# Order of the seven weight sums, the place of three loads, and the engine of some adds, in a one-layer streaming encoder on one core

## The chip, the cores and the metric

The kernel runs on one NeuronCore of one Trainium2 chip. The metric is the device time of one execution in microseconds (us). A core has five engines that work side by side, each through its own queue in order: TensorE (PE; its weight loads are shown as PEld), VectorE (DVE), ScalarE (ACT), GpSimd (POOL) and SyncE (SP). Nearly all transfers between the chip's main memory and the on-chip memory are issued from SP's queue.

## What is computed

One layer over 1024 prompt tokens and 64 sample tokens, handled as one matrix of 1088 columns: a combined projection, retention with four heads, sliding-window attention, a gated merge, cross-attention over 256 memory tokens, and a SwiGLU with an inner width of 2816, each with an RMS norm before it. All in float32. Cut to what matters here:

```
def mixer_prompt(h, g_attn, w_in, w_ret_out, w_swa_out, w_mix_out, sinks, bias, log_gamma):
    rq, rk, rv, rg, sq, sk, sv, ga, gb = in_proj(h, g_attn, w_in)
    q, k, v = retention_qkv(rq, rk, rv, pos)
    ret_state, o = lax.scan(lambda st, xs: retention_block(st, xs[0], xs[1], xs[2], log_gamma),
                            s0, (blk(q), blk(k), blk(v)))
    swa_o = swa_attend(q_s, band_blocks(k_s), band_blocks(v_s), bias, sinks, valid)
    y = merge_branches(ret_o, rg, swa_o, ga, gb, w_ret_out, w_swa_out, w_mix_out)

def swiglu(x, g_ffn, w_gate, w_up, w_down):
    hn = rms_norm(x, g_ffn)
    return (jax.nn.silu(hn @ w_gate) * (hn @ w_up)) @ w_down

hp = hp + y
hp = hp + cross_attn(hp, mk, mv, g_cross, w_cq, w_co)
hp = hp + swiglu(hp, g_ffn, w_gate, w_up, w_down)
```

## The kernel before

**Precision.** Each float32 operand is split in two halves (`split`, L122 to L124): ACT casts the high half (L123), DVE subtracts it from the source for the low half (L124). A product is then three matmuls: high by high, high by low, low by high (L212, L213 and L215 in `multiply`).

**Seven products instead of eight.** The large projections multiply a weight block of 2 by 2 parts with an activation block of 2 by 2 parts through seven products (`strassen`, L254). TensorE makes them in the order P1, P2, P6, P5, P7, P3, P4. Their activation operands are B11, B21, T2, T1, T3, B22 and T4, in that order: the B are parts of the activation, the T sums of such parts. A product of the full size is 24 matmuls of 128x128 by 272 columns, one of the last row group 18. The results are combined on DVE (`add` inside `strassen`, L259), and `emit`, which each caller writes, takes them out. In the profile the weight operands are called `wq`, the activation operands B, b or T (the digits of a name are left out there), and the result in PSUM `pq`.

**The weight operands.** `weight_ops` (L173) receives two tiles `raw` (two buffers in all; one holds a11 and a12, the other a21 and a22). Four sums are made in place on POOL (L190, L191, L193, L196), and each of the seven operands is split by `put` into a tile `wq` from `new_op` (five buffers, and a sixth one in a pool of its own from a certain point on). The order written is P1, P2, P7, P6, P5, P3, P4. P7 is a11 - a21; P6 is a22 - P7 and overwrites it, so it waits until P7 has been split; P5 is a21 + a22; P3 is a12 - P6. The argument `ahead` of `new_op` tells only the bookkeeping of the sixth buffer that products are used in another order than that of the splits. This function runs for each of 59 weight sets. The first pass of the projection and the first passes of two row groups use `plain` instead: eight products of the unsummed parts, with weights from `plain_weights`, and no sums.

**Order.** The program is traced once; a scheduler then orders the instructions of each queue by a simulated timeline, starting from the order of the text. `with tc.issue_after(ins):` makes what the block issues on the queue of `ins` follow `ins` on that queue.

**The start.** `start_phase` loads x in 16 pieces (`xr`, four buffers), scales them by the gain on ACT into `xg`, and makes the B and T operands. The values of head 0 (`values(first, 0, self.plain)`, L658) are the first product round, a `plain` one; its four results are stored to `d_qkv` through tiles `early`. The next line, L659, loads the two tiles of w_k for head 0 and makes their weight operands.

**The down projection.** `down` (L1556) multiplies w_down with the hidden values, which were stored earlier as operands in `d_op`. It runs over three row groups of 8, 8 and 6 blocks (gi = 0, 1, 2) and in each over four column pairs (m = 0, 2, 4, 6). In a pass the two `raw` tiles of w_down are loaded (`load_half`, L1594 to L1596), then the products follow. For gi = 0 and 1 the pass with m = 0 is a `plain` one, and after it the operands T2, T1, T3 and T4 of the group are loaded (`load_operand`, through tiles `hl` by `fetch`, L1548) for the passes after it. In the last pass of a group `refill` loads the next group's operand into each slot that has become free. Each result is added to y in `add` (L1563): what comes from PSUM on DVE (L1566), what comes from an on-chip sum (u1, u3, u5) on POOL (L1568) in the first two groups and on DVE in the last one.

Of the kernel before, what the change touches and what calls it, by code (L numbers as in the profile page):

```python
# [2 lines left out]

# [1 line left out]

# [16 lines left out]
KT = D // P  # L22
# [20 lines left out]
OPS = ("B11", "T1", "T2", "B21", "T3", "B22", "T4", "B12")  # L43
# [66 lines left out]
class Kernel:  # L110
# [8 lines left out]
    def store(self, out, in_):  # L119
        self.nc.sync.dma_start(out, in_)  # L120
# [20 lines left out]
            parts += [(q[:, 0, i:i + width], q[:, 1, i:i + width]) for i in range(0, w, width)]  # L141
        return parts

    def new_op(self, ahead=0):

        self.turns += 1
        turn = self.turns + ahead
        if self.sixth is not None and self.last_held < min(self.held):
            self.last_held = turn
            return self.sixth.tile([P, 2, 512], F32R, tag="wq", bufs=1, name="wq")  # L150
        self.held = sorted(self.held)[-4:] + [turn]
        return self.wp.tile([P, 2, 512], F32R, tag="wq", bufs=5, name="wq")
# [20 lines left out]
    def weight_ops(self, raws, n=512, skip=()):  # L173

        nc = self.nc
        half = [[raws[i][:, j * n:(j + 1) * n] for j in range(2)] for i in range(2)]
        (a11, a12), (a21, a22) = half
        add, sub = ALU.add, ALU.subtract
        w = {}

        def put(name, src):
            if name in skip:
                return
            q = w[name] = self.new_op({"P7": 2, "P6": -1, "P5": -1}.get(name, 0))
            self.split(src, q[:, 0, :n], q[:, 1, :n])

        tt = nc.gpsimd.tensor_tensor
        put("P1", a11)
        put("P2", a12)
        tt(out=a11, in0=a11, in1=a21, op=sub)  # L190
        tt(out=a21, in0=a21, in1=a22, op=add)  # L191
        put("P7", a11)
        tt(out=a11, in0=a22, in1=a11, op=sub)  # L193
        put("P6", a11)
        put("P5", a21)
        tt(out=a12, in0=a12, in1=a11, op=sub)  # L196
        put("P3", a12)
        put("P4", a22)
        return w
# [372 lines left out]
    def project_phase(self):  # L572
        nc, tc, io = self.nc, self.tc, self.io
        with ExitStack() as ctx:
# [7 lines left out]
            first = self.start_phase(sctx)  # L582
# [3 lines left out]
            half = lambda t: slice(t * HALF, (t + 1) * HALF)  # L586
            flat = lambda o: o.rearrange("p b c -> p (b c)")

            def staged():
                count[0] += 1  # L590
                return stage[(count[0] - 1) % len(stage)]

            def taken(ps, sb):
                o = staged()
                if sb is None:
                    nc.scalar.copy(o, ps)
                else:
                    nc.vector.tensor_tensor(out=o, in0=ps, in1=sb, op=ALU.add)  # L598
                return flat(o)
# [39 lines left out]

            def values(w, h, by=self.strassen):  # L640
                def emit(i, t, ps, sb):
                    self.store(self.d_qkv[2, 2 * h + i, :, half(t)], taken(ps, sb))
                by(w, self.ops, emit)

            pair = lambda w, h: self.load_ops([io[w][2 * h + i] for i in range(2)])
            def queries(p):
# [8 lines left out]
                        self.store(d[:, 9:17, :], r(o[:, 32:]))  # L655
                return put

            values(first, 0, self.plain)  # L658
            first = pair("w_k", 0)  # L659
            sctx.close()  # L660
            stage, count = self.stage_tiles(), [0]
            with ExitStack() as rctx:
# [24 lines left out]
            for idx, w, act in ((1, "w_ga", AF.Sigmoid), (0, "w_rg", AF.Silu), (2, "w_gb", AF.Sigmoid)):  # L687
                for m in range(0, KT, 2):
                    if (idx, m) == (1, 6):
# [4 lines left out]
                        op = ctx.enter_context(tc.tile_pool(name="op", bufs=1, reuse_waits="tile"))  # L694
# [4 lines left out]
                    put = lambda i, t, o, idx=idx, m=m, store=store: store(self.d_gate[idx][m + i, :, half(t)], o)  # L699
# [848 lines left out]
    def fetch(self, name, group):  # L1548
        n0 = sum(GROUPS[:group]) // 2
        for k in range(GROUPS[group] // 2):  # L1550
            self.pools = self.pools[1:] + self.pools[:1]
            a = self.pools[0].tile([P, HALF], F32, tag="hl", name="hl")
            self.load(a, self.d_op[OPS.index(name), n0 + k])
            yield a

    def down(self, starts):  # L1556
        nc, io = self.nc, self.io
        self.rings[0].next = (self.rings[0].next - 2) % KT
        stage = self.ring_tiles(0, 2, "y", F32)
        y = [self.rstd_f] + [stage[i // 2][:, i % 2, :] for i in range(4)]  # L1560
        y += [self.yp.tile([P, T], F32, name=f"y{i}") for i in range(3)]
        half = lambda m, t: y[m][:, t * HALF:(t + 1) * HALF]
        def add(m, i, t, ps, sb, by=nc.gpsimd):  # L1563
            v = half(m + i, t).rearrange("p (b c) -> p b c", b=2)
            if ps is not None:
                nc.vector.tensor_tensor(out=v, in0=ps, in1=v, op=ALU.add)  # L1566
            if sb is not None:
                by.tensor_tensor(out=v, in0=sb, in1=v, op=ALU.add)  # L1568

        begun = set()  # L1570

        def complete(m, c0, n):
            acc, o = self.rstd[:, c0:c0 + n], y[m][:, c0:c0 + n]
            if c0 not in begun:
                begun.add(c0)
                nc.scalar.activation(acc, o, AF.Square)
            else:
                sq = self.hl.tile([P, HALF], F32, tag="hl", name="sq")[:, :n]
                nc.scalar.activation(sq, o, AF.Square)
                nc.vector.tensor_tensor(out=acc, in0=acc, in1=sq, op=ALU.add)  # L1580

        def load_half(tile, m, a, b):
            self.load(tile.rearrange("p (k m) -> p k m", m=P), io["w_down"][m, :, a:b, :])

        for gi, g in enumerate(GROUPS):
            last = gi == len(GROUPS) - 1
            f0, n = starts[gi], g * P // 2
            for m in range(0, KT, 2):
                def emit(i, t, ps, sb, m=m):
                    add(m, i, t, ps, sb, nc.vector if last else nc.gpsimd)  # L1590
                    if last and t == 1:
                        complete(m + i, HALF, HALF)

                raws = [self.wp.tile([P, 1024], F32, tag="raw", bufs=2, name="raw") for i in range(2)]  # L1594
                for i in range(2):
                    load_half(raws[i][:, :2 * n], m + i, f0, f0 + g)  # L1596
                if m == KT - 4 and not last:
                    for name in ("B11", "B21" if gi == 0 else "T2"):
                        self.ahead[name, gi + 1] = list(self.fetch(name, gi + 1))
                if gi == 0:  # L1600
                    for i in range(2):
                        self.load(y[m + i], self.d_h[1][m + i])
                if m == 0 and not last:
                    self.plain(self.plain_weights(raws, n), self.ops, emit)
                    for name in ("T2", "T1", "T3", "T4"):
                        self.load_operand(name, gi)
                else:
                    w = self.weight_ops(raws, n, ("P2", "P4") if last else ())
                    if m == KT - 2 and not last:
                        self.refill = lambda name, gi=gi: self.turn(name, 1) if gi == 0 else self.turn_last(name)  # L1610
                    self.strassen(w, self.ops, emit, last)
                    self.refill = None
                    if m == 0:
                        for name in ("B21", "T4"):
                            self.load_operand(name, gi)
                if last and m == KT - 4:
                    nc.scalar.activation(self.root[:, 0, :1], self.rstd[:, HALF:HALF + 1], AF.Sqrt)
        rest = []
        for m in range(0, KT, 2):
            raw = self.wp.tile([P, 1024], F32, tag="raw", bufs=2, name="raw")  # L1620
            for i in range(2):
                load_half(raw[:, i * n:(i + 1) * n], m + i, f0 + g // 2, f0 + g)
            ring, slots = self.slots["B11" if m < 4 else "T1"]
            q = self.rings[ring].tile("wb", slot=slots[m // 2 % 2])
            self.last_queued = self.split(raw[:, :2 * n], q[:, 0, :2 * n], q[:, 1, :2 * n])
            rest += [(m + i, q[:, :, i * n:(i + 1) * n], self.ops[("B21", "T4")[i]]) for i in range(2)]
        self.finish(y, rest)
# [205 lines left out]
```

## Time and profile before

| | us |
|---|---|
| median of 3 runs | 2198.7 |
| lowest and highest | 2195.81, 2199.74 |
| the profiled execution's own time | 2201.3 |
| its span, first to last instruction | 2198.7 |

The profile is of one execution. A row of the timeline gives the start, the duration, the engine (a small q after it marks the engine's queue, as for an issued transfer), the line, the operation, the tiles as out<-in, the shapes and xcount; brackets tell how long the engine stood idle before it, and what ended that. A row of busy times by stretch gives the stretch and its length, then for PE, PEld, DVE, ACT and POOL the busy time and the number of instructions, then the mean granted clock of TensorE, the busy share of the transfer engines and GB/s. A row of the waits gives who waited for whom, the total, the number of times and the longest. A row of the chain of waits gives start, duration and what it was. A row of the groups gives the mean duration in ns after the busy time; a row of one line's instructions gives the shortest, the median and the longest.

### The profile page before, as it was taken

How to read it: one execution, taken by the hardware profiler on the slowest of the kernel's cores; microseconds unless marked ns; L12 is line 12 of the kernel's file. 1: busy time of each engine (PE TensorE's matmuls, PEld its weight loads, DVE VectorE, ACT ScalarE, POOL GpSimd, SP SyncE). 2: the span in 40 equal slices, each digit the busy share in tenths (PEclk: the TensorE clock that was granted, in tenths of full speed). 3: DMA queues.
4: the chain of work that ended last, by engine and by line, in shares of the span. 5: the costliest groups of instructions: out<-in, count | busy, mean ns of one | idle time of the engine just before them, and what ended most of it. 6: DMA issues, size and time to landing. Idle time of an engine off the chain costs nothing.

```text
span 2198.7 us, 41701 instructions
## 1 busy us (share of the span) xinstructions
PE 2151.3 (98%) x16389; PEld 2096.3 (95%) x16389; DVE 1566.3 (71%) x2650; ACT 877.2 (40%) x1898; POOL 658.1 (30%) x506
## 2 busy tenths in 40 slices
PE   8999999999999999999999999999999999999997
PEld 8999999999999997889999999999999999999997
DVE  8996968776677658766454565768777777777588
ACT  7343424344344456653233343333222222334243
POOL 1222333342344113330000000015556556424441
PEclk9999999999999999999999999999999999999999
DMA  5534354435354467327443111422342332475333
GB/s 199 167 123 128 99 150 123 133 112 158 104 161 161 166 207 243 114 80 220 121 156 115 40 49 58 149 82 90 124 147 88 104 123 91 131 291 164 96 105 119
DMA packets 181444, 290.83 MB, mean 132 GB/s; under 512 B 40290, under 2 KB 109314, under 8 KB 181250
## 3 DMA queue, kind: packets, MB, share of 16 engines
q1 hardware_dynamic: 176130, 278.18, 40.1%
q10 hardware_dynamic: 4608, 8.36, 1.0%
q8 instruction: 129, 2.11, 0.4%
q0 software_dynamic: 512, 1.64, 0.2%
q14 instruction: 65, 0.53, 0.1%
HBM read 196.95 MB, written 91.16 MB: 131 GB/s over the span
## 4 chain that ended last, share of the span: by engine, by line
PE 77%; DVE 11%; DMA 5%; issue 3%; ACT 3%; POOL 1%; SPq 0%; POOLq 0%; DVEq 0%; ACTq 0%
PE pq L215 15%; PE pq L213 15%; PE pq L212 15%; PE pd L156 7%; PE pd L158 7%; PE pd L157 7%; DVE wq L124 2%; DMA hl<-d_op 1%; PE pout L1038 1%; DVE T L124 1%; DVE B L124 1%; PE pss L970 1%; DMA raw<-w_k 1%; PE pp L1014 1%; DMA qs<-d_qkv 1%
## 5 line engine op out<-in xcount | busy, mean ns | idle before, releaser
L123 ACT CAST wq<-raw 128x512 fp32r<-128x512 f32 (+1 forms) x499 | 303.8, 614 | 593.2 <-PE pq L215 243.2
L124 DVE TENSOR_TENSOR wq<-raw,wq 128x512 fp32r<-128x512 f32 (+1 forms) x499 | 440.8, 886 | 137.5 <-ACT wq L123 135.7
L212 PE MATMUL pq<-T,wq 128*128 128x272 f32 x1832 | 491.7, 288 | 4.5 <-ACT wq L123 3.1
L213 PE MATMUL pq<-T,wq 128*128 128x272 f32 x1832 | 492.5, 289 | 0.0
L213 PE MATMUL pq<-B,wq 128*128 128x272 f32 x1592 | 430.1, 290 | 8.0 <-DVE B L124 8.0
L212 PE MATMUL pq<-B,wq 128*128 128x272 f32 x1592 | 427.6, 289 | 2.3 <-DVE stage L598 2.0
L215 PE MATMUL pq<-T,wq 128*128 128x272 f32 x1832 | 382.9, 289 | 0.0
L190 POOL TENSOR_TENSOR raw<-raw 128x512 f32<-128x512 f32 (+1 forms) x59 | 79.0, 1339 | 968.7 <-DVE rs_r L301 482.9
L212 PEld LDWEIGHTS pq<-T,wq 128*128 128x128 f32 x1832 | 344.9, 188 | 6.5 <-ACT wq L123 2.9
L213 PEld LDWEIGHTS pq<-T,wq 128*128 128x128 f32 x1832 | 344.8, 188 | 0.8 <-issue 0.7
L215 PE MATMUL pq<-B,wq 128*128 128x272 f32 x1592 | 333.4, 290 | 0.0
L213 PEld LDWEIGHTS pq<-B,wq 128*128 128x128 f32 x1592 | 300.9, 189 | 10.6 <-DVE B L124 9.7
L212 PEld LDWEIGHTS pq<-B,wq 128*128 128x128 f32 x1592 | 300.4, 189 | 3.2 <-ACT wq L123 2.7
L215 PEld LDWEIGHTS pq<-T,wq 128*128 128x128 f32 x1832 | 290.5, 190 | 0.5 <-issue 0.3
L215 PEld LDWEIGHTS pq<-B,wq 128*128 128x128 f32 x1592 | 253.4, 190 | 0.8 <-issue 0.8
L259 DVE TENSOR_TENSOR u<-pq,u 128x544 f32<-128x544 f32 x177 | 127.2, 719 | 99.1 <-PE pq L215 98.9
L193 POOL TENSOR_TENSOR raw<-raw 128x512 f32<-128x512 f32 (+1 forms) x59 | 83.5, 1415 | 125.7 <-DVE wq L124 120.6
L598 DVE TENSOR_TENSOR stage<-pq,u 128x544 f32<-128x544 f32 x112 | 80.2, 716 | 34.7 <-PE pq L215 31.7
L191 POOL TENSOR_TENSOR raw<-raw 128x512 f32<-128x512 f32 (+1 forms) x59 | 90.8, 1539 | 3.5
L196 POOL TENSOR_TENSOR raw<-raw 128x512 f32<-128x512 f32 (+1 forms) x59 | 83.0, 1406 | 4.4
L1486 POOL TENSOR_TENSOR stage<-stage,rstd_f 128x544 f32<-128x544 f32 x40 | 63.9, 1607 | 39.1 <-ACT stage L1485 39.1
L156 PE MATMUL pd<-xc,wq 128*128 128x256 f32 (+1 forms) x256 | 74.5, 291 | 0.0
(385 smaller groups left out, 4575.9 us busy)
## 6 DMA issues: line engine op xcount, KB each, us to landing
hl<-d_op SPq DMA_DIRECT2D x85, 272.0 KB, 4.3
d_qkv<-stage SPq DMA_DIRECT2D x44, 272.0 KB, 2.6
d_op<-stage SPq DMA_DIRECT2D x44, 272.0 KB, 2.1
d_op<-ht SPq DMA_DIRECT2D x44, 272.0 KB, 3.3
raw<-w_gate SPq DMA_DIRECT2D x22, 512.0 KB, 3.6
raw<-w_up SPq DMA_DIRECT2D x22, 512.0 KB, 4.0
raw<-w_down SPq DMA_DIRECT2D x16, 512.0 KB, 4.5
d_gate<-stage ACTq DMA_DIRECT2D x28, 272.0 KB, 3.0
```

Source lines behind the costliest of these rows:

```text
L123: self.last_cast = self.nc.scalar.copy(hi, src).ins
L124: return self.nc.vector.tensor_tensor(out=lo, in0=src, in1=hi.bitcast(F32), op=ALU.subtract).ins
L156: mm(ps, wh, xh, start=start, stop=False)
L157: mm(ps, wh, xl, start=False, stop=False)
L158: self.last_mm = mm(ps, wl, xh, start=False, stop=stop).ins
L191: tt(out=a21, in0=a21, in1=a22, op=add)
L193: tt(out=a11, in0=a22, in1=a11, op=sub)
L196: tt(out=a12, in0=a12, in1=a11, op=sub)
L212: mm(ps[:, c, :HC], w[:, 0, ks], x[:, 0, cs], start=start, stop=False)
L213: mm(ps[:, c, :HC], w[:, 0, ks], x[:, 1, cs], start=False, stop=False)
L215: self.last_mm = mm(ps[:, c, :HC], w[:, 1, ks], x[:, 0, c * HC:(c + 1) * HC], start=False, stop=stop).ins
L259: add = lambda out, a, b: nc.vector.tensor_tensor(out=out, in0=a, in1=b, op=ALU.add)
```

## The change

- `weight_ops`: the sums and splits are rewritten. a21 + a22 comes first and needs nothing but the second `raw` tile. P6 is then (a21 + a22) - a11, once P1 has been split. P3's sum follows, and P7 comes last as a22 - P6, once P6 has been split and P3's sum is made. The splits stand in the order of the products. There are four sums on POOL and seven splits as before. `new_op` loses its argument.
- The w_k loads of head 0 follow the first store of the values on SP's queue. For that, `values` keeps its stores (through `load`, which issues the same transfer and returns it).
- In the down projection, for gi = 0 and 1, the w_down loads of m = 2 follow the last load of operand T1 on SP's queue. `fetch` keeps each load, and the loop remembers T1's.
- In the last pass (m = 6) of the first two groups the adds of on-chip sums to y go from POOL to DVE: four in each pass, eight in all.

```
-    def new_op(self, ahead=0):
+    def new_op(self):
 
         self.turns += 1
-        turn = self.turns + ahead
+        turn = self.turns
...
-            q = w[name] = self.new_op({"P7": 2, "P6": -1, "P5": -1}.get(name, 0))
+            q = w[name] = self.new_op()
             self.split(src, q[:, 0, :n], q[:, 1, :n])
 
         tt = nc.gpsimd.tensor_tensor
         put("P1", a11)
+        tt(out=a21, in0=a21, in1=a22, op=add)
         put("P2", a12)
-        tt(out=a11, in0=a11, in1=a21, op=sub)
-        tt(out=a21, in0=a21, in1=a22, op=add)
+        tt(out=a11, in0=a21, in1=a11, op=sub)
+        put("P6", a11)
+        tt(out=a12, in0=a12, in1=a11, op=sub)
+        put("P5", a21)
+        tt(out=a11, in0=a22, in1=a11, op=sub)
         put("P7", a11)
-        tt(out=a11, in0=a22, in1=a11, op=sub)
-        put("P6", a11)
-        put("P5", a21)
-        tt(out=a12, in0=a12, in1=a11, op=sub)
         put("P3", a12)
         put("P4", a22)
...
-                    self.store(self.d_qkv[2, 2 * h + i, :, half(t)], taken(ps, sb))
+                    self.stores.append(self.load(self.d_qkv[2, 2 * h + i, :, half(t)], taken(ps, sb)))
...
+            self.stores = []
             values(first, 0, self.plain)
-            first = pair("w_k", 0)
+            with tc.issue_after(self.stores[0]):
+                first = pair("w_k", 0)
...
-            self.load(a, self.d_op[OPS.index(name), n0 + k])
+            self.loaded = self.load(a, self.d_op[OPS.index(name), n0 + k])
...
-                    add(m, i, t, ps, sb, nc.vector if last else nc.gpsimd)
+                    add(m, i, t, ps, sb, nc.vector if last or m == KT - 2 else nc.gpsimd)
...
-                for i in range(2):
-                    load_half(raws[i][:, :2 * n], m + i, f0, f0 + g)
+                with self.tc.issue_after(self.loaded) if m == 2 and not last else nullcontext():
+                    for i in range(2):
+                        load_half(raws[i][:, :2 * n], m + i, f0, f0 + g)
...
                         self.load_operand(name, gi)
+                        if name == "T1":
+                            behind = self.loaded
+                    self.loaded = behind
```

More of the change, by code (lines that the diff above doesn't have):

```diff
@@ L1 @@
 import math
-from contextlib import ExitStack, contextmanager
+from contextlib import ExitStack, contextmanager, nullcontext
 import numpy as np
```

## The prediction

> **What bounds the kernel now.** I began with the page's head and its busy times, then asked who TensorE waited for, then took busy times by stretch, and last read the timeline of each queue where TensorE had stood still.
>
> ```profile
> span 2198.7 us, 41701 instructions
> PE 2151.3 (98%) x16389; PEld 2096.3 (95%) x16389; DVE 1566.3 (71%) x2650; ACT 877.2 (40%) x1898; POOL 658.1 (30%) x506
> ```
> ```profile
> PE pq L213 <- DVE B L124: 8.0, 6, 2.9
> PE pq L212 <- ACT wq L123: 3.1, 3, 1.3
> ```
> ```profile
> 9.00:41.00 32.00, 27.98 (x201) 26.57 (x200) 31.07 (x46) 26.47 (x46) 3.33 (x2) 0.95 0.48 162
> 47.00:120.00 73.00, 68.68 (x530) 67.47 (x531) 69.85 (x121) 30.84 (x53) 20.27 (x14) 0.98 0.51 164
> 1540.00:1595.00 55.00, 55.00 (x444) 55.00 (x443) 42.08 (x51) 16.39 (x28) 30.26 (x22) 1.00 0.37 124
> 2015.00:2040.00 25.00, 21.25 (x145) 20.49 (x144) 20.55 (x26) 11.82 (x21) 10.43 (x7) 0.86 0.80 255
> 2135.00:2150.00 15.00, 13.09 (x89) 12.57 (x88) 14.06 (x23) 4.66 (x9) 5.42 (x5) 0.89 0.19 53
> ```
>
> TensorE bounds it: 47.4 us of the span are left without a matmul, and no schedule can win more than that and the half-speed clock behind the holes. The stretch 1540 to 1595 gives the full rate: 444 matmuls in 55 us, 0.124 us each, so a product of 24 matmuls takes 2.97 us and one of 18 (the last group) 2.23 us. By that rate the other stretches show what three places lose: 201 matmuls are 24.9 us of 32, a loss of 7.1 us at the start; 145 are 18.0 us of 25, a loss of 7.0 us where the down projection passes from its first row group to its second; 89 are 11.0 us of 15, a loss of 4.0 us in the last group. The second loss is 3.75 us of idle time and, with a mean clock of 0.86, 3.5 us of slowness. The two wait rows name the causes: operand halves that VectorE (DVE) finishes late, and split weights.
>
> **The start (gate on the w_k loads).**
>
> ```profile
> 12.79 0.38 SPq L117 DMA_DIRECT2D raw<-w_k  x1
> 14.49 0.76 SPq L117 DMA_DIRECT2D raw<-w_k  x1
> ```
> ```profile
> 32.05 0.83 SPq L120 DMA_DIRECT2D d_qkv<-early  x2
> ```
> ```profile
> 19.75 0.69 DVE L124 TENSOR_TENSOR wq<-raw,wq 128x512 fp32r<-128x512 f32 x1
> 20.36 0.72 DVE L1393 TENSOR_TENSOR xg<-xg 128x544 f32<-128x544 f32 x1
> 20.99 1.81 DVE L124 TENSOR_TENSOR T<-xg,T 128x544 fp32r<-128x544 f32 x1
> 22.73 1.78 DVE L124 TENSOR_TENSOR B<-xg,B 128x544 fp32r<-128x544 f32 x1
> ```
> ```profile
> 20.52 1.70 POOL L190 TENSOR_TENSOR raw<-raw 128x512 f32<-128x512 f32 x1 [20.07 <-DVE wq L124]
> 22.30 1.63 POOL L191 TENSOR_TENSOR raw<-raw 128x512 f32<-128x512 f32 x1
> ```
> ```profile
> 24.57 0.60 PE L213 MATMUL pq<-B,wq 128*128 128x272 f32 x1 [2.86 <-DVE B L124]
> 47.89 0.39 PE L212 MATMUL pq<-T,wq 128*128 128x272 f32 x1 [1.20 <-ACT wq L123]
> ```
>
> Today 1 MB of w_k goes out at 12.79 and 14.49 us, among the last loads of x. Its first split and its first two sums then fall between 19.75 and 24 us, and DVE's operands beside the sums take 1.81 and 1.78 us where a free one takes 0.72: 2.15 us lost, and 0.69 for the split. The B half that frees TensorE ends at 24.51; without these 2.84 us it would end at 21.67, and the 2.86 us hole begins at 21.71. After the change both loads stand on SP behind the first store (32.05). The x loads behind them come earlier, and nothing of w_k is on DVE or POOL before the store. DVE then has x work of its own (31.07 of 32 us busy), so I expect a second hole to stay, and take half of the 7.1 us.
>
> What the delay puts at risk is w_k itself. P1 of the first product round starts two products and the hole before 47.89: 47.89 - 1.20 - 5.94 = 40.75 us. From the store at 32.05:
>
> ```profile
> 72.49 5.04 DMA raw<-w_k
> ```
> ```profile
> 311.50 11.98 DMA raw<-w_k
> ```
>
> A w_k transfer of 5.04 us ends at about 37.5, and the split (0.69, and a cast of about that length before it) leaves 1.9 us to spare; store and P1 move together when the holes go. At 11.98 us it would be 5 us late. I take the first, as the x loads are out of the way by then. The 1.20 us hole at P6 should close: P6 then needs the early add and one subtraction, and no longer P7's split.
>
> What is won must still pass 47 to 120 us, where DVE is busy for 69.85 of 73 us. It has 3.15 us of slack there. So I count **3.0 us** for the start; bounds: 5 lost, 8.3 won.
>
> **The change of row group (gate on w_down, adds from POOL to DVE).**
>
> ```profile
> 2013.60 0.33 SPq L117 DMA_DIRECT2D raw<-w_down  x1
> 2014.23 1.82 SPq L117 DMA_DIRECT2D hl<-d_op  x1
> 2016.14 0.38 SPq L117 DMA_DIRECT2D raw<-w_down  x1
> ```
> ```profile
> 2020.86 1.82 DVE L124 TENSOR_TENSOR T<-hl,T 128x544 fp32r<-128x544 f32 x1 [0.21 <-ACT T L123]
> 2022.60 1.35 DVE L124 TENSOR_TENSOR B<-hl,B 128x544 fp32r<-128x544 f32 x2
> ...
> 2025.11 3.24 DVE L124 TENSOR_TENSOR B<-hl,B 128x544 fp32r<-128x544 f32 x2
> ```
> ```profile
> 2024.68 1.27 POOL L190 TENSOR_TENSOR raw<-raw 128x512 f32<-128x512 f32 x1 [2.59 <-DVE wq L124]
> 2025.92 1.84 POOL L1568 TENSOR_TENSOR y<-u,y 128x544 f32<-128x544 f32 x1
> ```
> ```profile
> 2026.59 0.39 PE L213 MATMUL pq<-B,wq 128*128 128x272 f32 x1 [2.33 <-DVE B L124]
> ```
> ```profile
> L1568 POOL TENSOR_TENSOR y<-u,y x24: 1348/1742/1841, 1962.3 to 2119.1; 128x544 f32<-128x544 f32 x24
> ```
>
> Two w_down loads for m = 2 stand between operand loads on SP, and their split and first sum meet the B halves: DVE's 1.82 and 3.24 us would be 0.72 and 1.35, 3.0 us too much, plus 0.69 for the split, as at the start. After the change these loads follow T1's last operand load; m = 2 comes only after the eight products of the plain pass, 23.8 us, which hides them. Eight adds (four in each of two groups) go from POOL (1.74 each) to DVE, at the 0.72 of the free 128x544 operation above. Before the hole two such adds cost DVE 1.4 us but no longer slow two others. The operand loads also get back the time of 1.05 MB, 4.1 us at the stretch's 255 GB/s; DVE idles 4.45 us in this stretch, so part is really loads. Of the 7.0 us I take **4.5**, bounds 0 and 7.0. In the first group the same gate meets no hole of size; I count nothing, bounds 1 us either way.
>
> **The last group (order of sums).**
>
> ```profile
> 2132.74 1.01 POOL L190 TENSOR_TENSOR raw<-raw 128x384 f32<-128x384 f32 x1 [6.77 <-DMA raw<-w_down]
> 2133.83 1.02 POOL L191 TENSOR_TENSOR raw<-raw 128x384 f32<-128x384 f32 x1
> 2136.61 1.41 POOL L193 TENSOR_TENSOR raw<-raw 128x384 f32<-128x384 f32 x1 [1.76 <-DVE wq L124]
> ```
> ```profile
> 2138.62 0.39 PE L212 MATMUL pq<-T,wq 128*128 128x272 f32 x1 [1.29 <-ACT wq L123]
> ```
>
> P6's weights come from the third sum, which waits for P7's split. In the new order they come from the second, ready at 2134.85, before TensorE asks (2138.62 - 1.29 = 2137.33). P7 is now later, but is used two products (4.5 us) after P6. The hole and its half clock go, 4.0 us at most; but DVE is busy 14.06 of 15 us there, so I count **2.0**, bounds 0 and 4.0.
>
> **Elsewhere** each set keeps four sums and seven splits, and TensorE runs at the full rate in stretches such as 1540 to 1595: nothing, with the second rival as the bound. The sum is 3.0 + 4.5 + 2.0 = 9.5 us: the profiled execution took 2201.3 us (span 2198.7), and 2191.8 would follow. It lies 2.6 us above the median of the runs shown, 2198.7, so the median is forecast at **2189 us**.
>
> [...] The holes above are 1.29 to 2.86 us, and the granted clock falls in each stretch that has them (0.95, 0.86, 0.89). [...]
>
> [...] The rows show operands of 0.72 us taking 1.8 us beside a POOL sum. [...]
>
> **Rivals.** *The next lateness* (0.16): the holes close, but DVE, with 3.15 us of slack from 47 to 120 and 0.94 in the last group, makes new ones. A third of the gain is left: 2198.7 - 3.2 = 2195.5. For it: DVE's 31.07 of 32. Against: two thirds of the start's loss is DVE time thrown away.
>
> *The P6 cast blocks ACT* (0.18, slower). P6's cast now needs two sums after the second raw tile where P7's needed one, and what is queued behind it on ACT (retention's ks, qs and vb casts, then DVE's low halves, then TensorE) waits one sum more.
>
> ```profile
> L191 POOL TENSOR_TENSOR raw<-raw 128x512 f32<-128x512 f32 x14 | 22.3, 1591 | 1.1
> L193 POOL TENSOR_TENSOR raw<-raw 128x512 f32<-128x512 f32 x14 | 20.0, 1430 | 48.3 <-DVE wq L124 45.7 <-DVE rr L301 2.6
> ```
> From 120 to 540 us there are 14 sets at 1.5 us. From 7 sets on the loss exceeds 9.5 us; at 12 of 14 it is 18, and 2198.7 - 9.5 + 18 = 2207. Against: ACT is busy 40%, and TensorE's waits for split weights are 3.1 us in the whole span.
>
> *w_k comes late* (0.06, slower): 5 us and half a clock window (1.7) at P1, and the sums' contention moved there, another 2 to 4: 2198.7 + 9 - 6.5 = 2201 to 2204, mostly above 2203.
>
> *No effect* (0.03): the written order already stands on SP at run time, 2198.
>
> *Idle time alone* (0.02): the half clock stays; 9.5 less half gives 2194.
>
> **Chances.** The forecast has 0.55, with a range of its own from 2180 (all bounds) to 2194 (half the sum). A measurement can tell 0.2%, 4.4 us. Faster takes 0.55, 0.06 of the next lateness and 0.02: 0.63. Within 0.2%: 0.10 and 0.03: 0.13. Slower: 0.18 and 0.06: 0.24. The range goes from 2180, all gains together, to 2206, short of the second rival's full price.
>
> **What would show it.** At the start: w_k issued after the first d_qkv store, no POOL sum before 30 us, DVE halves of 0.72 us there, and the 2.86 us hole gone or under 1 us. At the group change: w_down for m = 2 behind the T1 loads, y adds of the last pair on DVE, and at least 180 matmuls in a 25 us stretch where there were 145. In the last group: no hole at P6. The forecast is wrong if ACT waits on POOL sums double from 120 to 540 us with new TensorE holes there, or if the first P1 waits for w_k.

## The result and the profile after

The changed kernel takes 2186.8 us (median of 6 runs, 2186.2 to 2192.9) where the kernel before takes 2196.1 in the same series (6 runs, 2192.1 to 2199.7). The ratio is 0.9963, with a 95% interval of 0.9948 to 0.9977: 5.1 to 11.4 us faster. A second series gave 2187.5 us and 0.9947 (0.9930 to 0.9965). The forecast was 2189 us, so the total is right. Its parts are not: most of this document is about that. The profile shown next is of the slowest of the first six executions (2192.9 us), so its span lies above the median.

The head of the page of the changed kernel, and its busy times for the four lossy stretches of the prediction (columns as there):

```profile
span 2189.7 us, 41821 instructions
PE 2146.0 (98%) x16389; PEld 2089.9 (95%) x16389; DVE 1554.8 (71%) x2658; ACT 875.1 (40%) x1898; POOL 646.8 (30%) x498
```
```profile
9.00:41.00 32.00, 28.93 (x202) 27.02 (x201) 29.83 (x47) 28.01 (x50) 0.26 (x1) 0.95 0.50 160
47.00:120.00 73.00, 68.83 (x534) 67.78 (x534) 72.46 (x123) 30.26 (x54) 20.20 (x14) 0.98 0.48 158
2015.00:2040.00 25.00, 24.74 (x198) 24.46 (x197) 21.73 (x32) 14.53 (x26) 7.90 (x4) 1.00 0.71 245
2135.00:2150.00 15.00, 13.34 (x103) 12.73 (x102) 12.95 (x20) 5.90 (x10) 5.28 (x4) 1.00 0.26 80
```

The third row is the plain success: 198 matmuls where there were 145, and the full clock. The loads of w_down stand behind those of T1, an add to y and the B halves run at full speed on DVE, and TensorE waits for 0.26 us:

```profile
2020.54 0.33 SPq L117 DMA_DIRECT2D raw<-w_down  x1
```
```profile
2019.76 1.99 DVE L124 TENSOR_TENSOR B<-hl,B 128x544 fp32r<-128x544 f32 x3
2021.67 0.71 DVE L1570 TENSOR_TENSOR y<-u,y 128x544 f32<-128x544 f32 x1
```
```profile
2024.98 0.39 PE L213 MATMUL pq<-B,wq 128*128 128x272 f32 x1 [0.26 <-DVE B L124]
```

The first two rows say the opposite of what was hoped for: 202 matmuls for 201 at the start (a second profile of the same kernel has 216, with the full clock there), and VectorE (DVE) busy for 72.46 of 73 us behind it. The timeline of the start shows the w_k loads behind the first store of d_qkv, no sum on POOL before 40.74 us, and what TensorE (PE) still waits for:

```profile
32.54 0.33 SPq L117 DMA_DIRECT2D d_qkv<-early  x1
32.92 0.42 SPq L117 DMA_DIRECT2D raw<-w_k  x1
```
```profile
40.74 3.77 POOL L189 TENSOR_TENSOR raw<-raw 128x512 f32<-128x512 f32 x1 [40.29 <-DMA raw<-w_k]
```
```profile
26.97 0.40 PE L213 MATMUL pq<-B,wq 128*128 128x272 f32 x1 [1.69 <-DVE B L124]
47.85 0.39 PE L215 MATMUL pq<-T,wq 128*128 128x272 f32 x1 [0.50 <-DVE wq L124]
70.66 0.36 PE L212 MATMUL pq<-T,wq 128*128 128x272 f32 x1 [1.59 <-ACT xsq L476]
79.36 0.59 PE L212 MATMUL pq<-T,wq 128*128 128x272 f32 x1 [1.69 <-DVE u L259]
```

A hole can be followed from kernel to kernel by the number of the matmul that waited. The hole of 2.86 us (matmul 146) is gone, and in the place of the 1.20 us at P6 stand 0.50 four matmuls on. But the hole of 1.69 us at 25 us stood in the kernel before with 0.69 us, the one of 1.69 us at 78 us with 0.53, and the one of 1.59 us at 69 us is new. In the last row group nothing waits at P6; TensorE waits for DVE's adds instead, first one inside `strassen` and then two to y:

```profile
2140.68 0.36 PE L212 MATMUL pq<-T,wq 128*128 128x272 f32 x1 [0.50 <-DVE u L259]
2149.08 0.39 PE L212 MATMUL pq<-B,wq 128*128 128x272 f32 x1 [0.88 <-DVE y L1568]
2156.75 0.39 PE L156 MATMUL pq<-T,wb 128*128 128x272 f32 x1 [1.31 <-DVE y L1568]
```

**A ledger by matmul.** Each kernel here issues 16,389 matmuls in nearly the same order, so the start of the same matmul marks the same point of the work. The table gives the us between five such points, named by their time in the kernel before (matmuls 1,194, 3,193, 14,199 and 15,419, then the last matmul; the 7.2 to 8.8 us behind it are left out), for every profile of this study.

```
                                  0-165   165-430  430-1900  1900-2060  2060-end
before                           165.07    264.96   1470.00     160.01    131.29
changed kernel                   165.06    263.41   1469.96     153.30    130.46
all_again (changed, 2nd)         163.96    263.36   1467.40     153.86    130.37
a_only                           165.24    257.31   1468.06     158.69    130.39
b_only                           163.10    264.76   1469.98     154.80    131.85
c_only                           165.17    263.46   1469.19     154.23    129.53
d_only                           167.31    265.26   1469.92     159.72    130.59
without_order (A+B+C)            164.57    259.99   1468.51     153.02    129.53
order_last_only                  165.11    258.21   1469.36     152.28    129.32
without_wk_gate (B+C+D)          165.18    266.41   1466.74     154.70    130.03
after_bias_later                 163.45    257.96   1465.70     153.50    129.99
before_bias_later                163.02    258.51   1469.80     157.46    130.62
order_last_bias_later            162.36    258.04   1473.62     152.98    128.28
bias_later_no_wk_gate            167.16    258.94   1469.80     152.14    131.53
```

A is the gate on w_k, B the gate on w_down, C the y adds on DVE, D the order of sums and turns. Kernels with B or C alone have the instructions of the kernel before, in its order, up to 1900 us, so their first three columns are three profiles of one program. They differ by 2.1, 1.5 and 0.8 us, and the two profiles of the changed kernel differ by 2.6 us in the third: a difference of that size between two single profiles is no finding.

### The profile page after: what moved, and what is told of

Its sections match the earlier page's. It is cut to its first block, busy times and chain, and to the rows that moved or that the text cites. A ratio compares the mean times of both kernels' runs of the same rounds, so it can differ in the third digit from the quotient of the medians.

```text
span 2189.7 us, 41821 instructions
## 1 busy us (share of the span) xinstructions
PE 2146.0 (98%) x16389; PEld 2089.9 (95%) x16389; DVE 1554.8 (71%) x2658; ACT 875.1 (40%) x1898; POOL 646.8 (30%) x498
## 4 chain that ended last, share of the span: by engine, by line
PE 78%; DVE 10%; DMA 5%; issue 3%; ACT 2%; POOL 1%; SPq 0%; POOLq 0%; DVEq 0%; ACTq 0%
PE pq L215 15%; PE pq L213 15%; PE pq L212 15%; PE pd L156 7%; PE pd L158 7%; PE pd L157 7%; DVE wq L124 2%; DMA hl<-d_op 1%; PE pout L1040 1%; DVE B L124 1%; PE pss L972 1%; DMA raw<-w_k 1%; DMA qs<-d_qkv 1%; DVE T L124 1%; PE pp L1016 1%
## 5 line engine op out<-in xcount | busy, mean ns | idle before, releaser
L124 DVE TENSOR_TENSOR wq<-raw,wq 128x512 fp32r<-128x512 f32 (+1 forms) x499 | 434.7, 874 | 154.7 <-ACT wq L123 151.8
```

The lines of the kernel that those rows point to most:

```text
L124: return self.nc.vector.tensor_tensor(out=lo, in0=src, in1=hi.bitcast(F32), op=ALU.subtract).ins
```

## The experiments

**One part at a time.** The kernel before with one part of the change each; the edits are the hunks of the diff, here by their main lines.

```diff
+            with tc.issue_after(self.stores[0]):
+                first = pair("w_k", 0)
...
+                with self.tc.issue_after(self.loaded) if m == 2 and not last else nullcontext():
...
+                    add(m, i, t, ps, sb, nc.vector if last or m == KT - 2 else nc.gpsimd)
```

These are A, B and C, each with what the diff has beside it to name the stores and the last operand load; D is all of the diff in `weight_ops` and `new_op`. Each table below is a series of its own, with new runs of the kernel before, whose median goes from 2196.1 to 2198.6 us; from series to series the ratios compare better than the times.

> The kernel before with the w_k gate alone. Theory 'nothing is kept': the stretch 9 to 41 us wins 1 to 2 us, new holes on DVE between 60 and 120 us take it back, and by 165 us the lead over the kernel before is under 1 us; the time is 2195 to 2197. Prediction's theory: 3.0 us of lead at 120 us, kept to the end, 2193. Rival 'the order makes the holes': the holes of 1.6 to 1.7 us near 69 and 77 us come from the order of the sums and are not in this kernel, so its lead at 100 us is at least 1 us.

> The kernel before with the w_down gate alone (m = 2 behind T1's loads). Theory 'the gate does it': it alone wins 4 to 6.5 us at the change of row group, as the split and the sums of m = 2 leave the B halves, and the half clock near 2028 us goes; 2190 to 2192. Rival 'the adds do it': the y adds on POOL still slow the B halves to 1.8 us, a hole of over 1.5 us and its half clock stay, under 2 us is won.

> The kernel before with the y adds of the last pair of rows on VectorE alone. Theory 'the gate does it': the sums of m = 2 still meet the B halves, the hole near 2025 us stays over 1.5 us, the time is within 1.5 us of before. Rival 'the adds do it': 4 us or more won there.

> The kernel before with the new order of sums and turns alone. Theory 'given back': in the last row group the hole of 1.29 us at P6 and its half clock go (about 4 us of lead at matmul 16,100), and holes at y's adds on VectorE take back 2 to 3 us by the end; 1 to 1.5 us won in the down projection. Prediction's theory: 2.0 us won there. Second rival of the prediction: 120 to 540 us loses 5 us or more. Between 60 and 120 us: no hole over 1.5 us if the w_k gate makes those of the changed kernel.

| kernel | median, us (12 runs each; before: 2197.0) | ratio, 95% interval |
|---|---|---|
| a_only | 2190.8 (2188.5 to 2194.6) | 0.9971 (0.9958 to 0.9983) |
| b_only | 2193.2 (2189.3 to 2201.3) | 0.9978 (0.9964 to 0.9992) |
| c_only | 2190.6 (2186.1 to 2195.9) | 0.9967 (0.9954 to 0.9979) |
| d_only | 2202.8 (2195.3 to 2207.3) | 1.0020 (1.0006 to 1.0034) |

No theory held in full. A wins 6 us, twice the forecast, and yet stands where the kernel before stands at 165 us (165.24 against 163.0 to 165.2 of the same order without it): its gain lies between 165 and 430 us, where nothing was forecast. D makes the kernel slower. And of B and C, which share the change of row group, it is C that closes the hole. The stretch of the change in both, and in b_only the wait of TensorE and the DVE work before it:

b_only:

```profile
2010.00:2040.00 30.00, 27.45 (x220) 27.19 (x219) 26.93 (x36) 16.24 (x29) 11.07 (x7) 1.00 0.68 223
```
```profile
2017.73 3.80 DVE L124 TENSOR_TENSOR B<-hl,B 128x544 fp32r<-128x544 f32 x4
...
2022.08 2.48 DVE L124 TENSOR_TENSOR T<-hl,T 128x544 fp32r<-128x544 f32 x2
```
```profile
2025.25 0.39 PE L213 MATMUL pq<-B,wq 128*128 128x272 f32 x1 [2.55 <-DVE B L124]
```

c_only:

```profile
2010.00:2040.00 30.00, 30.00 (x242) 29.95 (x242) 26.94 (x40) 17.61 (x31) 5.91 (x4) 1.00 0.70 228
```
```profile
2021.65 2.92 DVE L124 TENSOR_TENSOR B<-hl,B 128x544 fp32r<-128x544 f32 x2
```

With the gate alone the adds stay on POOL, four B halves still take 3.80 us and two T halves 2.48, and a hole of 2.55 us remains. Over the whole change of row group TensorE's idle time falls from 4.4 to 2.6 us; the rest of the time is won because the half clock stays out (clock 1.00). That part may be chance: of the four profiles with neither B nor C, the kernel before has 6.8 us of half clock there, two have 3.4, and `before_bias_later`, a kernel that comes below, has none. With the adds moved, TensorE runs through all 30 us, though two B halves still take 2.92 us beside the sums of m = 2. Rival "the adds do it" holds for the hole. In the column 1900-2060 the four kernels with neither take 157.5 to 160.0 us, those with one 154.8 and 154.2, the eight profiles with both 152.1 to 154.7: two cures of one loss.

The start of d_only shows what the order costs there. Its sums on POOL:

```profile
20.66 1.30 POOL L189 TENSOR_TENSOR raw<-raw 128x512 f32<-128x512 f32 x1 [20.21 <-DMA xr<-xT]
22.04 1.63 POOL L191 TENSOR_TENSOR raw<-raw 128x512 f32<-128x512 f32 x1
26.90 1.62 POOL L193 TENSOR_TENSOR raw<-raw 128x512 f32<-128x512 f32 x1 [3.23 <-DVE wq L124]
```

In the old order two sums of w_k ran among the loads of x and the third at 42.95 us; in the new one three do, each beside a DVE operation of 1.8 us. The clock of its stretch 9 to 41 us is 0.84. No hole over 1.5 us stands between 60 and 120 us, and a_only has one (1.62 us at 78 us), as expected if A makes those of the changed kernel. Over all profiles, the hole at 78 us has 1.60 to 1.70 us in the seven with A, but also 1.61 in one without (`bias_later_no_wk_gate`), so it is not A's alone; the hole at 69 us stands only in the three with A and D.

**The whole, and the whole less one part.** `without_order` is A, B and C; `order_last_only` has the new order in the last row group only, `without_wk_gate` is B, C and D.

```diff
order_last_only, in weight_ops:
+        if skip:
...
+            put("P7", a11)
+        else:
             put("P2", a12)
             tt(out=a11, in0=a11, in1=a21, op=sub)
```

> The changed kernel once more, beside its variants: 2186 to 2189 us. Its profile shows how far the places of the holes vary between executions: theory 'the clock windows lie anew each time': the lead over the kernel before at 120 to 1900 us differs from the first profile's 1.6 by 1.7 us or a multiple; rival: it is the same within 0.5 us.

> The changed kernel with the old order of sums and turns (both gates and the moved adds alone). Theory 'the order costs only where w_k's first sums stand among the loads of x, and the gate takes them out': within 2 us of the changed kernel, 2185 to 2190. Rival 'the order costs everywhere': by the single parts (-6.2, -3.8, -6.4 us against 2197.0, the last two sharing one place of 7.0 us) 2181 to 2184, 4 us or more faster than the changed kernel.

> Both gates and the moved adds, and the new order in the last row group of the down projection alone. Theory: as the kernel without the order up to 2120 us; there the hole at P6 and its half clock go, and holes at y's adds return part, 1 to 2 us faster than without the order: 2180 to 2187, the fastest of all. Rival: the half clock at P6 falls in some executions only, and no difference shows.

> The changed kernel with w_k's loads where they stood. Theory 'the gate takes out what the order costs': three sums on POOL before 30 us, each beside VectorE operations of 1.8 us, two holes of 2 us or more and their half clock before 30 us; 6 to 9 us slower than the changed kernel, 2193 to 2196. Rival 'each part for itself': 3 us slower, 2190.

| kernel | median, us (before: 2198.6) | ratio, 95% interval |
|---|---|---|
| all_again | 2187.5 (6 runs) | 0.9947 (0.9930 to 0.9965) |
| without_order | 2184.4 (6 runs) | 0.9936 (0.9921 to 0.9952) |
| order_last_only | 2182.7 (6 runs) | 0.9927 (0.9910 to 0.9943) |
| without_wk_gate | 2194.1 (12 runs) | 0.9980 (0.9969 to 0.9992) |

The repeated profile is 3.2 us faster than the first over the whole span, 1.1 of it before 165 and 2.6 between 430 and 1900 us, and its lead over the kernel before at 1900 us is 5.3 where it was 1.6. The clock windows, in the first profile 3.413 us each at a clock of 0.50, do lie anew (28.0, 79.2 and 1376.3 us in the first profile, 335.6, 813.4 and 847.6 in the second), as the first theory said, but there are three in each, so their number does not make the 3.7 us. The largest piece, 2.2 us, lies between 1030 and 1210 us, where TensorE neither waits nor loses its clock; the last section comes back to it. Without the order the kernel is 3 us faster, between what theory and rival expected; the two intervals overlap, but the column 165-430 shows the place: 257.3 to 260.0 us in the kernels with A and the old order, 263.4 twice with A and D. The new order in the last group alone wins nothing in the last column (129.3 against 129.5 without it; 130.4 with the order everywhere). Its lead of 1.7 us in the medians lies inside the intervals. The kernel without A came in the time that the theory on it said, almost 7 us behind the whole, and with the two holes (2.88 and 3.08 us before 30 us). Yet by 165 us it is only 0.1 and 1.2 us behind the two profiles of the whole; 3.0 lie between 165 and 430 us, so the place is not the one that the theory named.

What do A win and D lose between 165 and 430 us? TensorE's longest wait there is at the scores of a retention block. SP's queue ahead of it, the transfers of that stretch (KB each, then the median us from issue to landing) and the wait, in the kernel before:

```profile
309.50 0.67 SPq L120 DMA_DIRECT2D d_rb<-rb  x1
311.50 4.95 SPq L117 DMA_DIRECT2D raw<-w_k  x2
```
```profile
d_rb<-rb SPq DMA_DIRECT2D x1, 1024.0 KB, 12.7
raw<-w_k SPq DMA_DIRECT2D x2, 512.0 KB, 11.0
```
```profile
338.24 0.36 PE L156 MATMUL pss<-qs,ks 128*128 128x256 f32 x1 [3.19 <-DVE kt L766]
```

in a_only:

```profile
298.38 0.67 SPq L120 DMA_DIRECT2D d_rb<-rb  x1
313.82 0.89 SPq L117 DMA_DIRECT2D raw<-w_k  x2
```
```profile
raw<-w_k SPq DMA_DIRECT2D x2, 512.0 KB, 5.0
```
```profile
333.12 0.35 PE L156 MATMUL pss<-qs,ks 128*128 128x256 f32 x1 [0.47 <-DVE kt L768]
```

and in the changed kernel:

```profile
308.20 0.67 SPq L120 DMA_DIRECT2D d_rb<-rb  x1
310.17 4.95 SPq L117 DMA_DIRECT2D raw<-w_k  x2
```
```profile
336.18 0.36 PE L156 MATMUL pss<-qs,ks 128*128 128x256 f32 x1 [2.44 <-DVE kt L768]
```

The transfer to d_rb stores the table of relative biases for the windowed attention, 1 MB, from `bias_table` (L549). It takes 12.7 us, and w_k, issued 2 us behind it, lands 11 us after its issue and not 5. The splits and sums of w_k come late to POOL and DVE (in the kernel before ACT's cast waits 9.4 us for the tile and POOL's first sum 9.0; in a_only 6.2 and 5.8), `kt` stands behind them on DVE, and the scores wait. The scheduler, which orders all queues anew for every edit, had put that store 15 us ahead of w_k in a_only, 2 us ahead of it in the kernel before, and, with D, 2 us ahead again. Nothing in the diff names this store.

**The bias store by itself.** The table is made one head later, in three kernels, so that its store leaves SP near 413 us.

```diff
-                    if h == 1:
+                    if h == 2:
                         self.later.append(self.bias_table)
...
+        with self.tc.issue_after(self.raw_load):
+            self.store(self.d_rb.rearrange("h (i c) -> h i c", c=512),
```

> The changed kernel with the table of relative biases (two small loads, a product, a copy, and the 1 MB store to d_rb) made one head later, so that the store leaves SP near 420 us and not just ahead of w_k's loads near 310. Theory 'the bias store holds w_k back, and the order of sums took back what the gate's new plan had won there': w_k lands 4 to 6 us after its issue where it took 12, the hole near 333 us falls from 2.4 to under 1 us, and the stretch 165 to 430 us takes 3 to 6 us less than the changed kernel's 263.4; 2181 to 2184. Rival 'another order of products does it': the hole moves or stays, within 1.5 us of the changed kernel.

> The kernel before with the bias table one head later and nothing of the change. Theory 'what the w_k gate alone wins (6.2 us) is this order': 165 to 430 us takes 258 to 261 us where it took 263.5 to 265.0; 3 to 6 us faster than before, 2191 to 2195. Rival 'the gate wins by the loads of x': under 1.5 us faster.

> Both gates, the moved adds, the new order in the last row group alone, and the bias table one head later. There the store already stood 10 us ahead of w_k, so the theory expects no more than 1.5 us either way: 2181 to 2184. Rival: the three d_qkv stores behind it were on the path, 2 us or more faster.

| kernel | median, us (before: 2197.3) | ratio, 95% interval |
|---|---|---|
| after_bias_later | 2181.4 (6 runs) | 0.9923 (0.9903 to 0.9942) |
| before_bias_later | 2193.7 (12 runs) | 0.9977 (0.9963 to 0.9991) |
| order_last_bias_later | 2182.7 (6 runs) | 0.9925 (0.9907 to 0.9943) |

In the changed kernel with the bias later, w_k lands in 3.4 us and the scores do not wait at all:

```profile
raw<-w_k SPq DMA_DIRECT2D x2, 512.0 KB, 3.4
```
```profile
330.99 0.28 PE L156 MATMUL pss<-qs,ks 128*128 128x256 f32 x1
```

The column 165-430 falls from 263.4 to 258.0 us with the change and from 264.4 (mean of three) to 258.5 without it, to the level of A with the old order. TensorE's idle time in it falls from 8.8 to 4.7 us in the changed kernel. That the table's own small product and copy left the stretch is not the reason: a_only keeps them there, 15 us earlier than w_k, and has 4.0 us. The theory holds, and the result is the fastest kernel of the study by the median, 5 to 6 us faster than the changed one. Where the store stood 16 us ahead already, moving it further changes nothing (2182.7 both times). With the store out of the way the new order costs nothing either: 2181.4 us with it everywhere, 2182.7 with it in the last group alone.

**What is left of the w_k gate.** The same edit, without the gate.

> The changed kernel with the bias table one head later, and w_k's loads where they stood before. It tells what the w_k gate is worth once the bias store no longer meets w_k at 310 us. Theory 'the gate itself is worth only what the new order would otherwise cost at the start': 165 to 430 us takes 257 to 260 us as with the gate, by 165 us it is 1 to 3 us behind, 2183 to 2185 against the 2181.4 with the gate. Rival 'the gate wins by what is left of the bias store': 263 us or more in that stretch, 2187 or more. Rival 'the prediction's 3.0 us, and what the order costs there beside it': 5 us or more behind by 165 us.

It took 2188.7 us (6 runs, 2183.5 to 2189.9; ratio 0.9953, 0.9939 to 0.9966), 7 us more than with the gate, which none of the three expected whole. The profiles place 3.7 of the 9.0 us between their spans before 165 us and 1.0 between 165 and 430. Another 4.1 lie between 430 and 1900 us, where profiles of one program differ by 2.6, and not by this much: one half-clock window more (1.7 us) and 2.1 us more of idle time. Profiles of one program differ by two windows and by 2.0 us of idle time there, so each piece could be chance, but the gate does reorder queues there too. Which it is stays open.

## Why the total was right and its parts were not

- **The start, 3.0 us forecast: 0 in the column.** By 165 us the kernels with the old loads stand at 163.0 to 165.2 (mean of four 164.1), the three with A and D at 163.5 to 165.1 (mean 164.2). What the prediction saw is there: the hole of 2.86 us gone, a second one kept, DVE halves of 0.72 us, w_k's first tile landed at 37.3 where 37.5 was said. The step that failed is that what is won there passes the stretch behind it ("It has 3.15 us of slack there"). The sums taken out of 20 to 24 us stand at 40.7 to 49.6 us, where the first alone holds POOL for 3.77, DVE fills 72.46 of 73 us, and the holes behind take back the 2.86 us: the next one grows by 1.0 us, the one at 78 us by 1.2, the new one at 69 us takes 1.6, and P6 returns 0.7. This is the first rival, in the place it named. A full DVE is not the whole reason, though: in a_only it is no fuller than before (69.90 us), and the lead is lost all the same, 1.0 and 1.1 us at the same two holes and 1.15 at P6, whose weights come no sooner (48.04 us against 47.89). The prediction counted one w_k transfer, but the second tile lands at 40.52 us (39.71 in a_only), and the first sum on POOL starts behind it. The gate's whole effect is 6 to 7 us in three comparisons. In the old order it is the bias store's new place, which "Elsewhere: nothing" ruled out: 7.1 us between 165 and 430 (264.4 less 257.3), where moving the store alone gives 5.9. Under D the gate does not move the store, and it wins the 2.4 us by which three kernels with D and the old loads are later at 165 us (mean 166.6), 1.0 to 3.0 us between 165 and 430, and a rest that stays open.
- **The change of row group, 4.5 us: 6.7** (160.01 less 153.30; 5.4 between the mean of the four profiles with neither B nor C, 159.0, and that of the two of the changed kernel, 153.6), within its bounds. The mechanism was right, and the size was off because a part was taken as "really loads": in c_only, with the loads where they were, TensorE idles for none of 30 us. The weight was on the wrong edit: the gate was costed as the cure and the adds as its price, but the adds alone close the hole. Each of the eight adds took 0.71 or 0.72 us on DVE in the changed kernel. An add of 1.8 us, as the rows of before have for operands beside a POOL sum (1.81 and 1.78), does not show; the slowest of these adds in any profile took 1.28 (c_only). In the first pass of the changed kernel no sum runs beside the adds; in the second one does, at 2112.16 us, and there the sum takes 1.99 us, against 1.02 of the one before it, while the add keeps its 0.71.
- **The last group, 2.0 us: 0.8 to 0.9** (131.29 less 130.46 and 130.37), and the new order need not be what won it: `c_only` and `without_order` have 129.5 without it. The hole at P6 and its half clock went as forecast, but neither was a steady loss: in the six profiles with the old order there the hole goes from none (with the adds moved) to 1.50 us, followed by one of 0.62 to 0.64, and four of the six have no half clock there. "DVE is busy 14.06 of 15 us there" was the right doubt, and half was too little of it: in the place of the holes at P6 stand those of 0.50, 0.88 and 1.31 us at DVE's adds.
- **The order of sums elsewhere, 0: it costs 3 us** (2187.5 against 2184.4 in one series), but not by the second rival. That rival put the loss at P6's cast on ACT between 120 and 540 us; with the bias store out of the way, D and the old order take the same 258 us between 165 and 430, and D is no slower in the whole (2181.4 against 2182.7). What D costs there is the store's old place.
- **w_k late, no effect:** the first P1 does not wait for w_k, and the time changed. The 1.7 us for half a clock window in the sum of "w_k comes late" is what the one from 24.59 to 28.00 us costs in the kernel before, 3.41 us at 0.50. **Idle time alone:** the clock of the third stretch rose from 0.86 to 1.00 as its holes went, which speaks against that rival; but `before_bias_later`, without B and C, keeps its clock there too, so it is not refuted.

So the 9.5 us met 9.1 between the two first profiles because 3.0 us too much at the start and 1.2 in the last group stood against 2.2 too little at the change of row group and 1.6 between 165 and 430 us, held at nothing. That they cancel is luck, and the 1.6 is hardly more than profiles of one program differ there (1.5). The key row was quoted in the prediction itself: a w_k load of 11.98 us at 311.50 beside one of 5.04. It was used as a bound for another load, and not asked why it was slow and who waited for it.

## What to carry to other kernels

Where a scheduler orders the queues, an edit moves transfers that it does not name: compare the order of each queue before and after, and price each large store by what is issued within its time (here 12.7 us, and w_k, issued 2 us into it, landed after 11 and not 5). A transfer that takes twice as long as its like (11.98 us beside 5.04) is a finding of its own, before any change. Where an engine fills the stretch behind a hole, as VectorE did here (69.85 of 73 us), count what is won in the hole as lost until a point behind that stretch shows it, and follow each hole by the number of the matmul that waited.

## What the hardware showed beside this

**The half clock fell on a lattice of 3.413 us in both kernels' profiles.** In the changed kernel, stretches of 3.4 us cut at the times where the clock falls:

```profile
24.60:28.00 3.40, 1.55 (x10) 1.33 (x11) 3.40 (x6) 3.40 (x8) 0.00 (x0) 1.00 0.01 3
28.00:31.40 3.40, 3.40 (x17) 3.40 (x17) 3.40 (x7) 3.40 (x8) 0.00 (x0) 0.50 0.00 0
68.90:72.30 3.40, 1.81 (x15) 1.67 (x14) 3.40 (x5) 2.67 (x5) 0.43 (x1) 1.00 0.10 26
72.30:75.70 3.40, 3.40 (x29) 3.40 (x29) 3.40 (x7) 1.17 (x2) 0.00 (x0) 1.00 0.75 233
75.80:79.20 3.40, 1.88 (x17) 1.79 (x15) 3.40 (x6) 1.29 (x2) 0.00 (x0) 1.00 0.92 278
79.20:82.60 3.40, 3.24 (x14) 3.24 (x15) 3.28 (x7) 1.14 (x2) 0.00 (x0) 0.50 0.96 341
1372.90:1376.30 3.40, 2.69 (x16) 2.12 (x16) 2.33 (x7) 1.19 (x5) 0.00 (x0) 1.00 0.58 171
1376.30:1379.70 3.40, 3.40 (x12) 3.40 (x12) 3.15 (x7) 2.85 (x6) 0.00 (x0) 0.50 0.49 167
```

The clock is 0.50 for one whole stretch, 3.413 us by the trace's own record, and then 1.00 again, and the falls at 28.0, 79.2 and 1376.3 us lie 15 and 380 times 3.413 us apart. In the kernel before the falls at 24.6, 116.8, 338.6, 816.5, 833.6, 2028.2 and 2140.9 us lie 27, 65, 140, 5, 350 and 33 times as much apart, and the clock is 0.50 for 3.413 us after each but the one at 2028.2, where it is for 6.827. TensorE was busy for 1.55, 1.88 and 2.69 us in stretches that were followed by a fall, for 1.81 in one that was not, so the busy time alone does not decide. The work around 1376 us is the same in both kernels, with the same two holes of 0.38 and 0.30 us. In the kernel before it came 3.2 us later, lay 0.2 us earlier against that profile's own steps of 3.413 us, and kept its clock, as it did in the second profile of the changed kernel, where it came 2.1 us earlier:

```profile
1372.90:1376.30 3.40, 3.24 (x24) 2.97 (x22) 1.28 (x4) 0.84 (x2) 0.00 (x0) 1.00 0.00 0
1376.30:1379.70 3.40, 2.87 (x17) 2.36 (x17) 2.44 (x8) 1.20 (x4) 0.00 (x0) 1.00 0.64 195
1379.70:1383.10 3.40, 3.40 (x21) 3.40 (x21) 3.15 (x7) 2.73 (x6) 0.00 (x0) 1.00 0.41 142
```

The same cluster of small holes cost 1.6 us in one profile (the lead of the changed kernel falls from 3.20 to 1.60 us there) and nothing in two others. That it depends on where the lattice cuts the cluster is the author's reading of these three profiles; no run shows it by itself.

**One stretch runs at one of two speeds.** From matmul 7,793 to 8,893, between about 1030 and 1210 us, the same work takes 178.6 us in seven of the fourteen profiles and 176.4 in the other seven. TensorE idles for nothing there, and the granted clock is 1.00. It is no matter of the program: the first profile of the changed kernel is among the slow seven and the second among the fast, and so are the kernel before (slow) and b_only (fast), which are one program up to there. The cause stays open.

**One sum on POOL took 20.7 us beside a busy VectorE.** The first sum of w_k took 1.70 us in the profile of before, and the DVE operation beside it 1.81. In c_only, whose start is the same program, it went the other way:

```profile
20.54 20.73 POOL L190 TENSOR_TENSOR raw<-raw 128x512 f32<-128x512 f32 x1 [20.09 <-DMA xr<-xT]
```
```profile
20.60:41.20 20.60, 16.67 (x124) 15.58 (x123) 19.52 (x31) 13.31 (x24) 20.60 (x1) 1.00 0.21 67
```

For 20.6 us DVE was busy for 19.52, each of its operations at full speed (0.69 to 0.72 us), and the one POOL sum did not end. What decides which of the two is slow was not shown.
